# Spare TensorE products at the start, and two loads on ScalarE's queue, in a two-layer hybrid block

## The chip, the cores and the metric

The kernel runs on one core of a Trainium2 chip. The metric is the device time of one execution in microseconds (us); the time of a kernel is the median of its runs. A core has a matrix engine (TensorE, PE in the profile; its weight loads stand apart as PEld), VectorE (DVE), ScalarE (ACT), GpSimd (POOL) and SyncE (SP), which issues the transfers from memory. Each engine takes its instructions strictly in the order in which they stand in its own line, and they wait for each other by semaphores.

## The reference

256 tokens of width 1024 go through two layers. Each layer is half a gated feed-forward step, a mixer (convolution with a state-space part in the first layer, dilated attention in the second) and another half feed-forward step, every one of them between two norms:

```python
for i in range(DEPTH):
    g = norm_g[i]
    h = h + 0.5 * rms_norm(swiglu(rms_norm(h, g[0]), ffn_w1[i, 0], ffn_w2[i, 0]), g[1])
    u = rms_norm(h, g[2])
    ...
    h = h + rms_norm(m, g[3])
    h = h + 0.5 * rms_norm(swiglu(rms_norm(h, g[4]), ffn_w1[i, 1], ffn_w2[i, 1]), g[5])
```

Only the beginning matters here: the norm of x with the weights `g[0]`, and the first two products of the first `swiglu`, with 256 gate and 256 up columns each.

## The kernel before, in words

**Work.** The tokens are two tiles of 128. All weights come from memory in float32, in units of 128 x 2048 (1 MB). Each unit is split into a high part `wh` (a copy in the type fp32r, by ScalarE) and a low part `wl` (the difference, by VectorE, or by GpSimd for some units), and so are the activations `x`. A product of two float32 matrices is then three products of parts: high x high, high x low, low x high (`mm3`, each 128x128 by 128x512).

**Beginning.** `run` loads the two halves of tile 0 of x, the identity matrix `ident` (64 KB), the first norm's weights `gain0` (4 KB, one column for each block of 128 features), the two halves of tile 1, and with `prefetch(2)` the first two weight units in pieces of 512 columns. All of these are issued by SyncE, one behind the other. Then `post_pre` norms each tile: ScalarE squares each half and sums it (`sumsq`; the squares themselves go to a tile `junk` that nobody reads), VectorE and GpSimd make the inverse root, VectorE scales (`y`), PE turns eight blocks of 128x128 by a product with `ident` (into the banks `t` and `c`, four each), ScalarE takes the high parts with the gain (`x<-t,gain`), and VectorE the low ones. The first two groups of products (banks `w`, two of them, one for each token tile) read the units 0 and 1, 24 products each. Behind each group stand an activation (`sg`) by ScalarE and a multiplication (`pt`) by VectorE that free the bank, and the third group needs the first one's bank. An activation of another kind needs a table load on ScalarE (`ACT_TABLE_LOAD`).

**Order.** The program is recorded first, and then a scheduler writes it: it plays the recorded operations through a table of costs (`cost`), takes on each engine the operation with the lowest rank among those that can start soonest, and also gives out the buffers. Ranks are the place in the recording, shifted by `moved(...)`. `FIRST_RANKS` shifts the conversions of the first two weight units. A waiting instruction holds up all that stands behind it on its engine. All instructions are issued from one line of the program (L633 in the profile of before), so its groups are told apart by the tiles' names: `w<-wh,x` is a product of `wh` and `x` into a bank `w`.

Of the kernel before, what the change touches and what calls it, by code (L numbers as in the profile page):

```python
# [13 lines left out]
BF16 = mybir.dt.bfloat16  # L14
# [5 lines left out]
P = 128  # L20
# [4 lines left out]
KB = D // P  # L25
# [17 lines left out]
AFTER = 0  # L43
WIDE = (6, 8)
FIRST_PIECES = (512, 512)
FIRST_RANKS = (-1950, -1950)
SECOND = 30
POOL_PIECE = 512
ON_POOL = (1, 1, 1)
SHARED = (0, 3)  # L50
SHARED_RANKS = (2000, 500)
# [156 lines left out]
C_ID, C_ORDER, C_TAB = 0, P, 3 * P  # L208
# [4 lines left out]
N_CHAN = 340  # L213
# [88 lines left out]
class Recorder:  # L302
# [182 lines left out]
    def one_schedule(self):  # L485
# [55 lines left out]
        while len(order) < len(ops):  # L541
            for e in stale:
                best[e] = choose(e)
            stale = set()
            picks = [(b[3], e) for e, b in best.items() if b]
            assert picks, "no operation can start"
            e = min(picks)[1]
            s, o = best[e][1:3]
            cands[e].remove(o)
            stale.add(e)  # L550
            for b in o.bufs:
                if b.slot is None:
                    kind = b.kind
                    times = sorted((t, i) for i, t in enumerate(kind.free_at) if t is not None)
                    b.slot = next(i for t, i in reversed(times) if t + GAP <= s)
                    kind.free_at[b.slot] = None
                    b.prev = kind.tenant.get(b.slot); kind.tenant[b.slot] = b
                    while kind.first < len(kind.bufs) and kind.bufs[kind.first].slot is not None:
                        kind.first += 1
                    left[b] = len(b.uses)  # L560
                    b.last = 0.0
            length = o.cost
            if e == "scalar" and o.table:
                if o.table != table:
                    length += TABLE_LOAD
                table = o.table
            if o.shares_port:
                length += max(0.0, port - s)
                held = s + length
            if e == "gpsimd":  # L570
                length += max(0.0, held - s)
                if o.takes_port:
                    port = s + length
            if o.before_pow and s > FIXED:
                quiet = s + length + QUIET
            free[e] = s + length
            if e == "sync":
                bus = max(bus, s + DMA_START) + o.tail
                end[o.index] = bus + DMA_LATENCY
            elif o.name == "dma_start":  # L580
                bus = max(bus, s + ADD_START) + o.tail
                end[o.index] = bus + ADD_LATENCY
            else:
                end[o.index] = s + length
            o.start, o.end = s, end[o.index]
            order.append(o)
            for b in o.bufs:
                b.last = max(b.last, end[o.index])
                left[b] -= 1
                if not left[b]:  # L590
                    b.kind.free_at[b.slot] = b.last
                    stale = set(free)
            for u in users[o.index]:
                n = ops[u]
                ready[u] = max(ready[u], end[o.index] + latency(o, n, n.deps[o.index]))
                waits[u] -= 1
                if not waits[u]:
                    cands[n.engine].append(n)
                    stale.add(n.engine)
# [55 lines left out]
def cost(op, out):  # L655

    kw = op.kw
    op.table = None
    op.shares_port = op.takes_port = False
    n = out.free_size() if isinstance(out, View) else 0  # L660
    if op.engine == "tensor":
        stationary = op.args[1]
        if op.name == "transpose":
            return 109.0, 0.0
        if stationary.ap.dtype == F32R:
            return n / 2.4 + 13.5 if n > 256 else 114.0, 0.0
        if PAIRED and (stationary.ap.ap[0][1] == 64 or stationary.free_size() == 64):
            return max(2 * n / 2.4 + 5.0, 110.0), 0.0
        return 2 * max(2 * n / 2.4 + 2.5, 112.0), 0.0
    psum = any(isinstance(a, View) and a.buf.kind.psum for a in (*op.args, *kw.values()))  # L670
    if op.engine == "scalar":
        op.table = TABLES.get(op.args[2])
        views = sum(isinstance(kw.get(k), View) for k in ("bias", "scale")) + ("accum_out" in kw)
        filled = 115.0 if isinstance(out, View) and out.buf.kind.psum else 0.0
        return 0.832 * n + (52.0 if psum else 96.0) + 93.0 * views + filled, 0.0
    if op.engine == "gpsimd":
        if op.name == "memset":
            return 100.0, 0.0
        if op.name == "dma_start":
            return ADD_START, n * P * 4 / ADD_RATE  # L680
        if n == 1:
            return 515.0, 0.0
        op.takes_port = True
        spread = any(isinstance(v, View) and v.ap.ap[-1][0] == 0 for v in kw.values())
        return (1.95 if spread else 2.26) * n + (10.0 if spread else 92.0), 0.0
    if op.engine == "vector":
        op.shares_port = not psum
        if op.name == "tensor_scalar" or op.name == "tensor_copy":
            return (0.52 if not psum else 1.04) * n + (70.0 if n < 64 else 130.0), 0.0
        if op.name == "scalar_tensor_tensor":  # L690
            return 1.03 * n + (130.0 if n > 64 and isinstance(kw.get("scalar"), View) else 75.0), 0.0
        if op.name == "bn_aggr":
            return 200.0, 0.0
        if op.name in ("tensor_reduce", "bn_stats"):
            n = op.kw["in_"].free_size()
        return 1.042 * n + 67.0, 0.0
    dst = kw["out"]
    cols = dst.free_size() if isinstance(dst, View) else kw["in_"].free_size()
    return 475.0, cols * P * 4 / 300.0
# [23 lines left out]
class Kernel:  # L723
# [58 lines left out]
        self.nc.scalar.activation(hi, src, AF.Copy)  # L782
        (engine or self.nc.vector).tensor_tensor(out=lo, in0=src, in1=hi.bitcast(F32), op=ALU.subtract)

    def prefetch(self, upto):
        while self.next_unit < min(upto, len(self.plan)):
            i = self.next_unit
            parts, whole, more, how, piece = self.plan[i]
            step = FIRST_PIECES[i] if i < len(FIRST_PIECES) else 2048

            def raw_of(name):
                key = (parts[name[0]], name[1])
                if key not in self.raws:
                    a = self.raws[key] = self.slot([P, 2048], tag="raw")
                    for c in range(0, 2048, step):
                        self.nc.sync.dma_start(out=a[:, c : c + step], in_=self.weights[key[0]][:, c : c + step])
                return self.raws[key]

            raw = raw_of(whole)
# [9 lines left out]
            with self.nc.moved(FIRST_RANKS[i] if i < len(FIRST_PIECES) else LATE):  # L809
                engine, step = (self.nc.gpsimd, POOL_PIECE) if i == 1 or i - self.hybrid_at in GPSIMD_UNITS else (self.nc.vector, piece)  # L810
                if i < len(FIRST_PIECES):
                    step = FIRST_PIECES[i]
# [109 lines left out]
    def sumsq(self, acc, src, scale):  # L922
        junk = self.slot([P, 512], BF16, "junk")
        self.nc.scalar.activation(junk, src, AF.Square, scale=scale, accum_out=acc)

    def post_pre(self, t, y, half, gpost, gpre, xT, last=False):

# [5 lines left out]
    def _post_pre(self, t, y, half, gpost, gpre, xT, last):  # L933
        nc = self.nc
        f = 2.0 if half else 1.0
        h = self.h[t]
        hs = [slice(hf * 512, (hf + 1) * 512) for hf in range(2)]
# [8 lines left out]
        s2 = self.sm(2) if gpre is not None else None  # L946
        for hf in range(2):
            if y is not None:
                nc.vector.scalar_tensor_tensor(out=h[:, hs[hf]], in0=yg[hf], scalar=r, in1=h[:, hs[hf]], op0=ALU.mult, op1=ALU.add)
            if last:  # L950
                nc.sync.dma_start(out=self.out[t * P : (t + 1) * P, hs[hf]], in_=h[:, hs[hf]])
            if gpre is not None:
                self.sumsq(s2[:, hf : hf + 1], h[:, hs[hf]], 1 / 32.0)
                if y is not None:
                    nc.vector.tensor_tensor(out=yg[hf], in0=h[:, hs[hf]], in1=gpre[:, hs[hf]], op=ALU.mult)
        if gpre is None:
# [718 lines left out]
    def run(self):  # L1675
# [6 lines left out]
            (self.ffn, True),  # L1682
        ]
        xT = self.transposed_tile()
        load = self.nc.sync.dma_start
        for hf in range(2):
            c = slice(hf * 512, (hf + 1) * 512)
            load(out=self.h[0][:, c], in_=self.x[0:P, c])
        load(out=self.ident, in_=self.consts[:, C_ID : C_ID + P])
        load(out=self.gain0, in_=self.in_small[0][:, N_CHAN : N_CHAN + KB])  # L1690
        for hf in range(2):
            c = slice(hf * 512, (hf + 1) * 512)
            load(out=self.h[1][:, c], in_=self.x[P : 2 * P, c])
# [68 lines left out]
```

## Time and profile before

| | |
|---|---|
| median of three runs | 1057.73 us (1057.48, 1057.73, 1058.43) |
| the profiled execution | 1058.54 us, of which 1056.8 us from the first to the last instruction |
| PE busy | 1040.7 us (98%) |
| DVE, ACT, POOL busy | 934.9, 706.4, 193.1 us |
| read from memory | 194.5 MB, 185 GB/s over the span |

The timeline's rows give the start and the length of a merged row of equal instructions, the engine, the operation with its tiles, and the count; in brackets the idle time before it and who ended it. A row's length runs from the first start to the last end, and products overlap, so a product's step is read from the starts of rows. Times count from the first instruction.

### The profile page before, as it was taken

To read this page: it belongs to the slowest core of one execution; us is meant where nothing else is said; L and a number is where in the kernel's file an instruction comes from. 1 tells how busy PE (TensorE), PEld (TensorE's weight loads), DVE (VectorE), ACT (ScalarE), POOL (GpSimd) and SP (SyncE) were. 2 spreads that over 40 slices of the span, in tenths; PEclk is the share of its full clock that TensorE was granted. 3 is DMA by queue.
4 is the path that set the end of the run, shared out by engine and by line. 5 is a ranking of instruction groups with operands and counts; after the bars stand their busy time and mean duration, and the time that the engine had idled before them with its cause. 6 is when DMAs were issued, how large, how long until landed. Compare 5 with 4: busy or idle time off the path is not lost.

```text
span 1056.8 us, 14986 instructions
## 1 busy us (share of the span) xinstructions
PE 1040.7 (98%) x5426; PEld 871.1 (82%) x5426; DVE 934.9 (88%) x1525; ACT 706.4 (67%) x1327; POOL 193.1 (18%) x171
## 2 busy tenths in 40 slices
PE   6999999999999999999999999999999999999997
PEld 5888888899878888888888888888888788888886
DVE  4799997789999899999979999997688769999993
ACT  6756766679776685756766667586577657575671
POOL 2410000199995030000003000000000413000000
PEclk9999999999999999999999999999999999999999
DMA  9572657455332633754743557393755231475451
GB/s 334 202 276 108 252 200 278 160 172 183 124 104 96 239 120 139 263 222 173 288 173 138 182 216 262 109 345 136 266 180 180 100 121 60 158 261 216 162 199 40
DMA packets 30633, 196.51 MB, mean 186 GB/s; under 512 B 3680, under 2 KB 4576, under 8 KB 8032
## 3 DMA queue, kind: packets, MB, share of 16 engines
q1 hardware_dynamic: 30560, 195.57, 50.8%
q8 instruction: 42, 0.69, 0.3%
q14 instruction: 31, 0.25, 0.1%
HBM read 194.51 MB, written 1.05 MB: 185 GB/s over the span
## 4 chain that ended last, share of the span: by engine, by line
PE 94%; ACT 3%; DVE 1%; issue 1%; DMA 1%; SPq 0%; DVEq 0%; POOLq 0%; POOL 0%; ACTq 0%
PE w L633 40%; PE a L633 32%; PE t L633 12%; PE c L633 10%; ACT wh L633 1%; ACT s L633 1%; DMA raw<-in_weights 1%; ACT junk L633 0%; DVE wl L633 0%; ACT L633 0%; SPq L633 0%; DVE s L633 0%; ACT x L633 0%; DVE h L633 0%; DVE c L633 0%
## 5 line engine op out<-in xcount | busy, mean ns | idle before, releaser
L633 ACT ACTIVATE wh<-raw 128x512 fp32r<-128x512 f32 (+1 forms) x626 | 452.5, 775 | 145.0 <-DVE raw L633 49.3
L633 DVE TENSOR_TENSOR wl<-raw,wh 128x512 fp32r<-128x512 f32 (+1 forms) x554 | 483.5, 920 | 35.2 <-ACT wh L633 32.5
L633 PE MATMUL a<-wh,s 128*128 128x512 f32 x800 | 255.6, 391 | 0.0
L633 PE MATMUL w<-wh,x 128*128 128x512 f32 x600 | 197.5, 401 | 1.7 <-ACT x L633 1.2
L633 PEld LDWEIGHTS a<-wh,s 128*128 128x128 f32 x800 | 149.6, 188 | 32.2 <-ACT s L633 0.9
L633 PE MATMUL a<-wl,s 128*128 128x512 f32 x400 | 155.8, 390 | 0.0
L633 PE MATMUL w<-x,wh 128*128 128x512 f32 (+1 forms) x512 | 143.8, 348 | 0.1
L633 POOL TENSOR_TENSOR m<-m,mhalf 128x1 f32<-128x1 f32 x28 | 16.6, 594 | 694.0 <-DVE m L633 694.0
L633 PEld LDWEIGHTS w<-wh,x 128*128 128x128 f32 x600 | 112.5, 189 | 27.0 <-ACT x L633 1.9
L633 PE MATMUL w<-wl,x 128*128 128x512 f32 x300 | 118.9, 397 | 0.0
L633 PE MATMUL w<-x,wl 128*128 128x256 f32 x400 | 112.5, 281 | 0.0
L633 DVE TENSOR_TENSOR raw<-raw,raw 128x1024 f32<-128x1024 f32 (+1 forms) x104 | 110.0, 1087 | 0.1
L633 PEld LDWEIGHTS w<-x,wh 128*128 128x128 f32 x512 | 88.5, 189 | 12.2 <-DVE pt L633 0.5
L633 POOL TENSOR_TENSOR wl<-raw,wh 128x512 fp32r<-128x512 f32 x72 | 90.9, 1303 | 18.5 <-ACT wh L633 18.4
L633 PEld LDWEIGHTS a<-wl,s 128*128 128x128 f32 x400 | 75.1, 188 | 15.1
L633 PE MATMUL w<-wh,s 128*128 128x512 f32 x264 | 86.8, 390 | 0.0
L633 PEld LDWEIGHTS w<-x,wl 128*128 128x128 f32 x400 | 75.5, 189 | 1.3 <-issue 1.0
L633 PEld LDWEIGHTS w<-wl,x 128*128 128x128 f32 x300 | 56.9, 190 | 12.1 <-issue 0.6
L633 PEld LDWEIGHTS w<-wh,s 128*128 128x128 f32 x264 | 49.6, 188 | 10.7 <-ACT s L633 0.5
L633 PE MATMUL t<-x,wh 128*128 128x512 f32 x160 | 57.9, 397 | 0.0
L633 PE MATMUL c<-x,wh 128*128 128x512 f32 x160 | 56.6, 393 | 0.0
L633 DVE SCALAR_TENSOR_TENSOR t<-cv,chan,t 128x254 f32<-128x254 f32 (+29 forms) x112 | 52.3, 467 | 3.6 <-ACT t L633 3.2
(202 smaller groups left out, 1554.7 us busy)
## 6 DMA issues: line engine op xcount, KB each, us to landing
raw<-in_weights SPq DMA_DIRECT2D x176, 1024.0 KB, 4.9
g<-in_gains SPq DMA_DIRECT2D x11, 512.0 KB, 4.8
raw<-in_weights SPq DMA_DIRECT2D x8, 256.0 KB, 5.9
h<-in_x SPq DMA_DIRECT2D x4, 256.0 KB, 3.3
out<-h SPq DMA_DIRECT2D x4, 256.0 KB, 2.0
g<-in_consts SPq DMA_DIRECT2D x3, 192.0 KB, 2.4
chan<-in_chan SPq DMA_DIRECT2D x1, 170.0 KB, 9.4
order<-in_consts SPq DMA_DIRECT2D x1, 128.0 KB, 9.6
```

Of the source, the lines that this page charges most:

```text
L633: o.ins = f(*[real(a) for a in o.args], **{k: real(a) for k, a in o.kw.items()})
```

## The change

- `SPARES`: PE gets products of a 128x128 bf16 tile `spare` of zeros, which GpSimd clears at the start, into a bank `a` that nobody reads. Thirty come first, with the tile as both operands. After the first square of tile 0 come 8, after the second 12, after the second square of tile 1 another 6; these read 128 columns of the square's `junk` tile as an operand, so that they wait for the square, and a later square that takes the same `junk` buffer waits for them.
- `ident` and `gain0` are issued from ScalarE's own queue (`nc.scalar.dma_start`), ahead of its table load, and no longer by SyncE.
- `FIRST_RANKS`: the conversions of unit 1 get the rank shift -600 in place of -1950. `prefetch` has a new argument `beside` that no call uses. The table of costs learns the new kinds.

```diff
-FIRST_RANKS = (-1950, -1950)
+FIRST_RANKS = (-1950, -600)
...
+SPARES = (30, 8, 12, 0, 6)
...
     def sumsq(self, acc, src, scale):
         junk = self.slot([P, 512], BF16, "junk")
         self.nc.scalar.activation(junk, src, AF.Square, scale=scale, accum_out=acc)
+        return junk[:, 0:P]
+
+    def spares(self, count, moved):
+
+        for _ in range(count):
+            self.nc.tensor.matmul(self.bank[:, 0:P], self.spare, moved, start=True, stop=True)
...
-                self.sumsq(s2[:, hf : hf + 1], h[:, hs[hf]], 1 / 32.0)
+                junk = self.sumsq(s2[:, hf : hf + 1], h[:, hs[hf]], 1 / 32.0)
+                if y is None:
+                    self.spares(SPARES[1 + 2 * t + hf], junk)
...
         xT = self.transposed_tile()
+        self.spare = self.keep("spare", [P, P], BF16)
+        self.nc.gpsimd.memset(self.spare, 0.0)
+        self.bank = self.ps([P, 512], "a")
+        self.spares(SPARES[0], self.spare)
         load = self.nc.sync.dma_start
         for hf in range(2):
             c = slice(hf * 512, (hf + 1) * 512)
             load(out=self.h[0][:, c], in_=self.x[0:P, c])
-        load(out=self.ident, in_=self.consts[:, C_ID : C_ID + P])
-        load(out=self.gain0, in_=self.in_small[0][:, N_CHAN : N_CHAN + KB])
+        beside = self.nc.scalar.dma_start
+        beside(out=self.ident, in_=self.consts[:, C_ID : C_ID + P])
+        beside(out=self.gain0, in_=self.in_small[0][:, N_CHAN : N_CHAN + KB])
```

How the instructions stand now. PE, from the program's start to the first products, before (`t` and `c` are the turns of a tile's first and second half, `w` the products; the first two rows are tile 0, `t_228` is tile 1):

```order
L633 MATMUL t_186<-ident_64,y_0_69 128x128 x4
L633 MATMUL c_193<-ident_64,y_1_70 128x128 x4
L633 MATMUL w_207<-wh_123,x_73 128x512
L633 MATMUL w_207<-wl_74,x_73 128x512
L633 MATMUL w_207<-wh_123,x_73 128x512 x2
L633 MATMUL t_228<-ident_64,y_0_77 128x128 x4
```

PE at the same place now; of each run of spares (30, 8, 12, 6 pairs of a weight load and a product) one pair is shown:

```order
L634 LDWEIGHTS spare_124
L634 MATMUL a_165<-spare_124 128x128
...
L634 MATMUL a_165<-junk_67,spare_124 128x128
...
L634 MATMUL a_165<-junk_69,spare_124 128x128
L634 MATMUL t_240<-ident_63,y_0_71 128x128 x4
...
L634 MATMUL a_165<-junk_235,spare_124 128x128
L634 MATMUL c_260<-ident_63,y_1_73 128x128 x4
L634 MATMUL w_269<-wh_123,x_75 128x512
```

The first turn has fifty spares ahead of it. The turns of tile 1 moved too: the first four from behind four products to behind eight, and the second four from behind 26 products to behind 15. Now ScalarE, from its first instruction on, before:

```order
L633 ACT_TABLE_LOAD
L633 ACTIVATE junk_67,m_0_147<-h_0_63 128x512
...
L633 ACTIVATE wh_123<-raw_66 128x512
L633 ACTIVATE x_73<-t_186,gain_0_132 128x128 x2
L633 ACTIVATE x_76<-t_186,gain_0_132 128x128 x2
L633 ACTIVATE wh_123<-raw_66 128x512 x3
L633 ACTIVATE x_79<-c_193,gain_0_132 128x128 x2
```

And ScalarE now:

```order
L634 DMA ident_63<-in_consts 128x128
L634 DMA gain_0_134<-in_chan 128x8
L634 ACT_TABLE_LOAD
L634 ACTIVATE junk_67,m_0_149<-h_0_64 128x512
...
L634 ACTIVATE wh_123<-raw_66 128x512
L634 ACTIVATE x_75<-t_240,gain_0_134 128x128 x2
L634 ACTIVATE wh_123<-raw_66 128x512
L634 ACTIVATE x_78<-t_240,gain_0_134 128x128 x2
L634 ACTIVATE wh_123<-raw_66 128x512 x2
```

Two issues stand ahead of the table load, and the second weight piece (`wh<-raw`) stands between the high parts of x. VectorE follows that order, before:

```order
L633 TENSOR_TENSOR wl_74<-raw_66,wh_123 128x512
L633 TENSOR_SCALAR y_0_77<-h_0_65,m_3_201 128x512
L633 SCALAR_TENSOR_TENSOR x_73<-t_186,gain_0_132,x_73 128x128 x2
L633 SCALAR_TENSOR_TENSOR x_76<-t_186,gain_0_132,x_76 128x128 x2
L633 TENSOR_TENSOR wl_74<-raw_66,wh_123 128x512
```

And VectorE now:

```order
L634 TENSOR_TENSOR wl_76<-raw_66,wh_123 128x512
L634 TENSOR_SCALAR y_0_77<-h_0_65,m_3_254 128x512
L634 TENSOR_TENSOR wl_76<-raw_66,wh_123 128x512
L634 SCALAR_TENSOR_TENSOR x_75<-t_240,gain_0_134,x_75 128x128 x2
L634 TENSOR_TENSOR wl_76<-raw_66,wh_123 128x512
```

A second low weight piece stands ahead of the first low parts of x. Behind the first 48 products the order is the same but for some 50 instructions on PE, ScalarE and VectorE that changed places with a near neighbour.

More of the change, by code (lines that the diff above doesn't have):

```diff
@@ L576, in one_schedule @@
             free[e] = s + length
-            if e == "sync":
+            if e == "sync" or e == "scalar" and o.name == "dma_start":
                 bus = max(bus, s + DMA_START) + o.tail
@@ L664, in cost @@
             return 109.0, 0.0
+        if stationary.ap.dtype == BF16:
+            return 107.0 if op.args[2].buf.kind.name == "spare" else 60.0, 0.0
         if stationary.ap.dtype == F32R:
@@ L670, in cost @@
     psum = any(isinstance(a, View) and a.buf.kind.psum for a in (*op.args, *kw.values()))
+    if op.name == "dma_start" and op.engine == "scalar":
+        return 450.0, out.free_size() * P * 4 / 300.0
     if op.engine == "scalar":
@@ L783, in split, with prefetch @@
         (engine or self.nc.vector).tensor_tensor(out=lo, in0=src, in1=hi.bitcast(F32), op=ALU.subtract)
-    def prefetch(self, upto):
+    def prefetch(self, upto, beside=None):
         while self.next_unit < min(upto, len(self.plan)):
@@ L795, in raw_of @@
                     for c in range(0, 2048, step):
-                        self.nc.sync.dma_start(out=a[:, c : c + step], in_=self.weights[key[0]][:, c : c + step])
+                        (beside if beside and not c else self.nc.sync.dma_start)(out=a[:, c : c + step], in_=self.weights[key[0]][:, c : c + step])
                 return self.raws[key]
```

## The prediction

> **What bounds the kernel now.** I read the page first: its first row gives the span, its second and fourth the busy time of TensorE (PE) and VectorE (DVE).
>
> ```profile
> span 1056.8 us, 14986 instructions
> ...
> PE 1040.7 (98%) x5426; PEld 871.1 (82%) x5426; DVE 934.9 (88%) x1525; ACT 706.4 (67%) x1327; POOL 193.1 (18%) x171
> ```
>
> PE is idle for 1056.8 - 1040.7 = 16.1 us. The windows tell where: busy time of PE, PEld, DVE, ACT and POOL in turn, then the granted clock, the DMA share and GB/s.
>
> ```profile
> 0.00:25.06 25.06, 16.80 (x65) 13.00 (x65) 11.87 (x31) 17.02 (x41) 6.45 (x11) 1.00 0.91 331
> 25.06:50.00 24.94, 24.81 (x127) 20.84 (x128) 18.99 (x25) 19.34 (x35) 11.64 (x10) 1.00 0.61 215
> 50.00:100.00 50.00, 50.00 (x253) 42.32 (x252) 48.28 (x54) 30.47 (x43) 4.86 (x3) 1.00 0.48 178
> 100.00:170.00 70.00, 69.95 (x337) 58.55 (x336) 67.23 (x89) 49.48 (x75) 0.00 (x0) 1.00 0.67 254
> 1050.50:1056.80 6.30, 0.00 (x0) 0.00 (x0) 2.23 (x4) 0.69 (x2) 0.55 (x1) 0.69 0.22 83
> ```
>
> Of the 16.1 us, 8.26 lie before 25.06 and 6.30 behind the last product; 1.5 are left for 1025 us between. So whatever the first 25 us are shortened by ends the run earlier by as much, if nothing behind takes it back. The chain that ended last shows what that beginning waits for, in order of time:
>
> ```profile
> 2.58 0.43 SPq L633
> ...
> 3.53 5.29 DMA raw<-in_weights
> ...
> 9.78 2.38 PE w L633 x4
> ...
> 20.78 2.08 ACT wh L633 x4
> ...
> 22.87 1.28 ACT L633
> 24.17 0.39 ACT sg L633
> ...
> 24.58 0.43 DVE pt L633
> ...
> 25.06 5.10 PE w L633 x21
> ```
>
> SyncE's issues, the first weight piece (landed at 8.82), conversion, products; then from 20.78 a detour over ScalarE's conversions, its table load and the gate, until the third group of products starts at 25.06. The timeline of PE shows that the first products also run slowly (start, time of the row, count at the end):
>
> ```profile
> 6.78 1.11 PE L633 MATMUL t<-ident,y 128*128 128x128 f32 x4 [6.78 <-DVE y L633]
> 7.69 1.06 PE L633 MATMUL c<-ident,y 128*128 128x128 f32 x4
> ...
> 13.24 1.48 PE L633 MATMUL w<-wh,x 128*128 128x512 f32 x3
> 14.53 0.98 PE L633 MATMUL w<-wl,x 128*128 128x512 f32 x2
> 15.34 0.62 PE L633 MATMUL w<-wh,x 128*128 128x512 f32 x2
> ...
> 19.00 0.60 PE L633 MATMUL c<-ident,y 128*128 128x128 f32 x4
> 19.36 0.70 PE L633 MATMUL w<-wh,x 128*128 128x512 f32 x2
> 19.89 0.39 PE L633 MATMUL w<-wl,x 128*128 128x512 f32 x1
> ```
>
> From 13.24 to 14.53 three products take 0.43 us each. In a later stretch this window, PE alone, holds 19 that start in it (a twentieth began before): 18 steps in 4.10 us, 0.228 each.
>
> ```profile
> 20.12:24.24 4.12, 4.12 (x20) 1.00 1.00 373
> ```
>
> Turns go from 0.23 (four from 6.78 to 7.69) to 0.109 ((19.89 - 19.00 - 2 x 0.228) / 4). Both halve at about 15.3: a clock that is let go then, though the clock column already reads 1.00 over 0 to 25.06. It came 8.5 us after the first turn and 5.5 after the first product.
>
> **The change part by part.** The sum is made inside the profiled execution (1058.54 us, span 1056.8, so 1.7 outside), and asks when the third group of products, now at 25.06, can start.
>
> *Two loads to ScalarE's queue.* Rows of SyncE's queue, of ScalarE's table load and of the squares:
>
> ```profile
> 1.64 0.42 SPq L633 DMA_DIRECT2D ident<-in_consts  x1
> 2.11 0.43 SPq L633 DMA_DIRECT2D gain<-in_chan  x1
> ...
> 0.73 1.28 ACT L633 ACT_TABLE_LOAD   x1 [0.73 <-PEq L1752]
> 3.77 0.63 ACT L633 ACTIVATE junk<-h 128x512 bf16<-128x512 f32 x1 [1.76 <-DMA h<-in_x]
> 5.99 0.63 ACT L633 ACTIVATE junk<-h 128x512 bf16<-128x512 f32 x1 [0.74 <-DMA h<-in_x]
> ```
>
> Everything behind them on SyncE is issued 2.58 - 1.64 = 0.94 us earlier. The bytes stay, so the first weight piece comes 0 to 0.94 earlier than 8.82. I take 0.65: the second tile of x waits for its issue (0.74 idle before the square at 5.99), but the small packets still pass. So it lands at 8.17. On ScalarE the two issues push the table load to 0.73 + 0.94 + 1.28 = 2.95; the square at 3.77 hides that by 0.8. Identity is wanted at 6.78, the gains at 8.7; both land in time even at a landing time of 4 us. Two weight pieces now wait on the semaphores of these loads; their bytes queue behind earlier pieces, cost nothing.
>
> *Spares.* GpSimd clears the constant behind its first memset at 0.73, so PE starts at 1.1. No bf16 product of 128 columns is in the trace. Bounds: a quarter of the slow 512-column step, 0.43 / 4 = 0.107 us, and the slow f32 turn, 0.23. [...] Then 30 end at 4.3; 8 wait for the first square (3.77 + 0.63 = 4.4) and end at 5.3, 12 end at 6.6, ahead of the turn at 6.78: nothing is moved by them. [...] What they bring is the clock: with the two delays above it is free at 1.1 + 5.5 = 6.6 to 1.1 + 8.5 = 9.6.
>
> A wait is added: ScalarE's third square waits until PE has read the junk tile, 5.3 to 5.6, and behind it queue the fourth square and all conversions. The square now starts at 5.99, so it is covered as long as 38 spares stay under 0.13 each.
>
> *The new order of conversions.* After the first piece (rows: conversion 8.84, high parts of x 9.38; VectorE 9.51, 10.12, 10.54):
>
> ```profile
> 8.84 0.63 ACT L633 ACTIVATE wh<-raw 128x512 fp32r<-128x512 f32 x1 [1.38 <-DMA raw<-in_weights]
> 9.38 1.13 ACT L633 ACTIVATE x<-t,gain 128x128 fp32r<-128x128 f32 x4
> 9.51 0.69 DVE L633 TENSOR_TENSOR wl<-raw,wh 128x512 fp32r<-128x512 f32 x1 [1.80 <-ACT wh L633]
> 10.12 0.48 DVE L633 TENSOR_SCALAR y<-h,m 128x512 f32<-128x512 f32 x1
> 10.54 1.13 DVE L633 SCALAR_TENSOR_TENSOR x<-t,gain,x 128x128 fp32r<-128x128 f32 x4
> 10.95 1.22 PE L633 MATMUL w<-wh,x 128*128 128x512 f32 x2
> 14.28 5.04 POOL L633 TENSOR_TENSOR wl<-raw,wh 128x512 fp32r<-128x512 f32 x4 [5.87 <-ACT wh L633]
> 19.64 1.14 ACT L633 ACTIVATE x<-c,gain 128x128 fp32r<-128x128 f32 x4 [2.85 <-PE c L633]
> ```
>
> The third product needs the low parts of x: 10.95 - 8.84 = 2.11 us after the conversion. One low weight piece now stands ahead of them on VectorE (0.61, from 9.51 to 10.12), so 2.72; from 8.19 that is 10.9. Behind it everything is there when its turn comes: 46 products x 0.228 = 10.49 and 8 turns x 0.109 = 0.87, so the third group at 22.26. GpSimd starts its four low pieces at about 12.95 (8.19 + 4 conversions x 0.52 + 8 high parts x 0.25 + one conversion) and ends them at 18.0; the last is wanted at 19. The turns of the second tile's second half stand far earlier, so ScalarE no longer idles 2.85 us for them. Its conversions of the third unit wait for PE to leave the first unit's buffer: 10.9 + 24 x 0.228 + 0.87 + 0.4 = 17.6, then 2.1, 1.3, 0.4 and 0.4 for conversions, table, gate and multiply: 21.8. So the gate is no longer waited for, by 0.4 us.
>
> Sum: 22.26 - 25.06 = **-2.8 us**: 0.65 from the loads, some 2.4 from the clock (ten products at 0.2 and four turns at 0.1), 0.6 from the gate, less 0.85 for the longer wait for the third product.
>
> *Behind it* the order is nearly the same. The four weight tiles issued from here on have slack:
>
> ```profile
> 19.49 8.86 SPq L633 DMA_DIRECT2D raw<-in_weights  x4
> 31.81 0.62 ACT L633 ACTIVATE wh<-raw 128x512 fp32r<-128x512 f32 x1
> ...
> raw<-in_weights SPq DMA_DIRECT2D x6, 1024.0 KB, 7.6
> ```
>
> 19.49 + 7.6 = 27.1 against a use at 31.81: 4.7 us, more than the 2.8.
>
> **Against the runs shown** (1057.48 to 1058.43, median 1057.73) the profiled execution is 0.81 slow. Is that noise in both kernels, the change gives 1057.73 - 2.8 = 1054.9; is it something that the change removes, 1058.54 - 2.8 = 1055.7. I forecast the middle, **1055.3 us**. A difference under 0.2% (2.1 us) is what a measurement of this kernel can't tell from none.
>
> **The rivals.**
>
> *The clock comes as late as now.* The constant is zero and PE may not count such products as work. Then PE runs at half its pace from 10.9 to 15.3 and loses 2.2 of these 4.4 us: -2.8 + 2.2 = -0.6 from the median, about 1057.1. For it: the first turns, too, did not free the clock for 8.5 us. Against: the 30 spares are dense, which nothing before 9.78 was.
>
> *The clock's phase.* The release may fall at another point in each execution. The slowest of four times is the profiled one; if its 0.81 is a late release, the median loses less now, and the gain against it is 2.8 - 0.8 = 2.0: 1055.7. For it: the four times spread by 1.06 us. Against: nothing says that the spread is in the beginning. [...] No row here shows a second phase.
>
> *The spares stand in the way (slower).* They are in PE's line ahead of the turn, and ScalarE's squares wait for them. At 0.23 each with a late clock 50 end at 1.1 + 11.5 = 12.6, the six others and the eight turns put the first product at 15.8, 6.0 later than 9.78; then come 5.5 us of slow products (13), 35 x 0.228 and 0.87: 30.2, that is +5 us, 1062.8. It decides from about 0.14 us a spare (5 / 56 = 0.09 less than 0.23) if the clock is late too. Against: 0.23 is an f32 price.
>
> *VectorE takes it back.* It is idle for only 1.7 of 50 us from 50 and 2.8 of 70 us from 100. If it can't move forward, PE meets its waits again, and 0 to 2 us of the gain stay: about 1056.9. Against: VectorE is idle for 6 of 25 us from 25 on, and the transfers have slack.
>
> **How the numbers follow.** Forecast 0.58, phase 0.12, late clock 0.13, VectorE 0.09, spares in the way 0.06, something else on the slow side 0.02. The forecast's own bounds: the first piece 0 to 0.94 earlier (gain 2.15 to 3.1), a spare at 0.16 (turn at 9.1, some 0.9 less), both readings of the 0.81. The range is 1053.9 to 1057.2, which takes in the late clock. Faster: nearly all of the forecast and part of the phase, 0.60; same 0.32; slower 0.08.
>
> **What would show it.** Right: spares at 0.107 from 1.1, halving before 9.6; turns at 6.8 to 7.0; first piece converted at about 8.2; no step over 0.25 among the products from 10.9 on; the third group at 22.3 with no wait for the gate; and the same 2.8 us at 100 us as at the end. Wrong: products at 0.43 behind 11; a first turn behind 7.5; a first conversion still at 8.8; new waits for VectorE's low parts between 50 and 170.

## The result and the profile after

| | before | after |
|---|---|---|
| median | 1057.36 us (10 executions, 1056.29 to 1058.54) | 1055.39 us (10 executions, 1054.84 to 1057.03) |
| ratio, 95% interval | | 0.9981 (0.9972 to 0.9989) |
| the profiled execution, its span | 1058.54, 1056.8 us | 1055.28, 1053.5 us |

The change makes the kernel faster by 1.97 us in the median, 0.19%, just under what the prediction called telling; the interval excludes a ratio of 1. One of the eleven executions of a later kernel, first30, took 1713.98 us at a granted clock of 0.567; its median below is that of the other ten. Between the two profiled executions the difference is larger, 3.3 us. This gap between 2.0 and 3.3 is the first thing to explain.

The page after, first row and PE's row:

```profile
span 1053.5 us, 15099 instructions
...
PE 1042.8 (99%) x5482; PEld 873.3 (83%) x5482; DVE 934.0 (89%) x1525; ACT 706.0 (67%) x1327; POOL 193.5 (18%) x172
```

PE is idle for 10.7 us instead of 16.1, but 3.4 + 1.7 + 0.5 us of its busy time is now spares. The windows, cut at the third group of products as before (at 21.83 now instead of 25.06):

```profile
0.00:21.83 21.83, 19.19 (x120) 15.83 (x121) 12.22 (x32) 17.31 (x41) 6.64 (x12) 1.00 0.93 338
21.83:50.00 28.17, 27.84 (x141) 23.16 (x140) 21.52 (x29) 22.08 (x38) 11.21 (x10) 1.00 0.63 242
...
1047.20:1053.50 6.30, 0.00 (x0) 0.00 (x0) 2.23 (x4) 0.69 (x2) 0.55 (x1) 0.72 0.22 83
```

25.06 - 21.83 = 3.23 us are won in the beginning, and the span is 3.3 shorter: what happens between changes little in sum, and the end (6.30 us without PE, as before) nothing. The start of PE's products, compared one by one in the two traces, leads by 3.39 us at 27 us, 2.86 at 107 and 3.32 at the last product. The timeline of PE, after:

```profile
1.03 3.38 PE L634 MATMUL a<-spare 128*128 128x128 bf16 x30 [1.03 <-POOL spare L634]
4.56 1.69 PE L634 MATMUL a<-junk,spare 128*128 128x128 bf16 x20 [0.15 <-ACT junk L634]
6.76 0.66 PE L634 MATMUL t<-ident,y 128*128 128x128 f32 x4 [0.51 <-DVE y L634]
7.45 0.49 PE L634 MATMUL a<-junk,spare 128*128 128x128 bf16 x6
7.78 0.61 PE L634 MATMUL c<-ident,y 128*128 128x128 f32 x4
8.52 0.50 PE L634 MATMUL w<-wh,x 128*128 128x512 f32 x1
8.99 0.50 PE L634 MATMUL w<-wl,x 128*128 128x512 f32 x1
10.28 0.73 PE L634 MATMUL w<-wh,x 128*128 128x512 f32 x2 [0.79 <-DVE x L634]
10.85 0.39 PE L634 MATMUL w<-wl,x 128*128 128x512 f32 x1
```

Thirty spares take 3.38 us, the next twenty only 1.69; the record of the granted clock begins at 5.47 us (before: at 15.28). The first turns take 0.66 us instead of 1.11, the first product 0.50 instead of 0.80, and from 10.28 on the longest product step is 0.31 (at 14.21). The chain that ended last in the first 30 us:

```profile
0.73 3.23 DMA ident<-in_consts
...
4.82 5.07 DMA raw<-in_weights
9.88 0.35 DVE x L634
...
10.28 1.66 PE w L634 x6
```

From 10.28 on it is PE alone: the detour over the table load and the gate, which stood in the chain before, is gone. Ahead of that the chain has to be read with care. It puts the low parts of x at 9.88 down to the weight piece that was issued at 4.82. But that piece lands only at 10.75; it shares a semaphore with the gains, and those landed at 4.68. Rows of VectorE and, the last, of ScalarE:

```profile
9.27 0.69 DVE L634 TENSOR_TENSOR wl<-raw,wh 128x512 fp32r<-128x512 f32 x1
9.88 0.60 DVE L634 SCALAR_TENSOR_TENSOR x<-t,gain,x 128x128 fp32r<-128x128 f32 x2
```

```profile
9.13 0.62 ACT L634 ACTIVATE x<-t,gain 128x128 fp32r<-128x128 f32 x2
```

What ends just before the low parts of x is VectorE's second low weight piece (9.96, the instructions overlap a little) and ScalarE's second pair of high parts (9.75).

### The profile page after: what moved, and what is told of

Read it like the earlier page. It is cut to its first block, busy times and chain, and to the rows that moved or that the text cites. A ratio compares the mean times of both kernels' runs of the same rounds, so it can differ in the third digit from the quotient of the medians.

```text
span 1053.5 us, 15099 instructions
## 1 busy us (share of the span) xinstructions
PE 1042.8 (99%) x5482; PEld 873.3 (83%) x5482; DVE 934.0 (89%) x1525; ACT 706.0 (67%) x1327; POOL 193.5 (18%) x172
## 3 DMA queue, kind: packets, MB, share of 16 engines
HBM read 194.51 MB, written 1.05 MB: 186 GB/s over the span
## 4 chain that ended last, share of the span: by engine, by line
PE 96%; DVE 1%; ACT 1%; DMA 1%; issue 1%; SPq 0%; DVEq 0%; POOLq 0%; POOL 0%; ACTq 0%
PE w L634 41%; PE a L634 33%; PE t L634 12%; PE c L634 9%; DVE wl L634 1%; DMA raw<-in_weights 0%; ACT wh L634 0%; ACT junk L634 0%; DMA ident<-in_consts 0%; ACT s L634 0%; DVE s L634 0%; ACT L634 0%; DVE h L634 0%; DVE raw L634 0%; SPq L634 0%
```

## Experiments

**The kernel before, twice more.** No edit. Is the late release of the clock (15.28 us) a property of the kernel or of that execution?

> The kernel before once more, for one profile. My theory (the clock's phase): the slow steps of 0.43 us end at another point than 15.3, anywhere between 11.9 and 15.3, and the third group starts the earlier the sooner they end, 23.5 to 25.1; the span moves with it, by about 0.4 us for each us. Rival (noise elsewhere): third group at 25.0 to 25.1 again, and a span that differs from 1056.8 does so behind 25 us.

> The same kernel and the same expectations as the first look: by the phase theory a third point of release, with the third group between 23.5 and 25.1 and a span that follows it; by the rival the third group at 25.0 to 25.1.

Measured: 1056.33 and 1057.70 us. The timeline of PE in the first of the two:

```profile
9.36 0.68 PE L633 MATMUL w<-wl,x 128*128 128x512 f32 x1
9.93 1.18 PE L633 MATMUL w<-wh,x 128*128 128x512 f32 x2
10.94 0.60 PE L633 MATMUL t<-ident,y 128*128 128x128 f32 x4
...
22.66 0.50 PE L633 MATMUL w<-wh,x 128*128 128x512 f32 x1 [0.46 <-DVE pt L633]
```

Products and turns halve at 10.92 here, at 13.67 in the second repeat, at 15.28 in the profile of before. The third group starts at 22.66, 24.27 and 25.06, the spans are 1054.2, 1055.7 and 1056.8. So the beginning of the kernel before differs by 2.4 us from execution to execution, and the whole run follows it. The conversion of the first weight piece also starts at different times: 7.83, 8.76 and 8.84 us.

**Loads alone, spares alone.** The first has no spares, the second has the loads on SyncE again; both keep the new ranks, and the scheduler was left to lay out the rest. `...` marks lines left out, here and below.

```diff
 loads_alone
-SPARES = (30, 8, 12, 0, 6)
+SPARES = (0, 0, 0, 0, 0)
...
-        self.spare = self.keep("spare", [P, P], BF16)
-        self.nc.gpsimd.memset(self.spare, 0.0)
-        self.bank = self.ps([P, 512], "a")
-        self.spares(SPARES[0], self.spare)
 spares_alone
-        beside = self.nc.scalar.dma_start
+        beside = load
```

> The change without its spare products (no constant, no bank for them); identity and gains still go by ScalarE's queue, and the new rank shift stays. My theory: two parts, the clock and the earlier pieces. Without spares the clock is let go late, at some point between 11.9 and 15.3 us that differs from run to run; the first weight piece is converted at 7.6 as in the changed kernel, not at 8.84; the third group of products starts at 22 to 23.6, against 25.06 in the profile of before and 21.83 in that of the changed kernel. Time between the two kernels: 0.7 to 1.5 us under before, ratio 0.9987 to 0.9993, so within 0.2%. Rival, that the spares bring all of it: first piece near 8.8 or third group at 24.5 or later, ratio 0.9997 to 1.0005. Rival, that the loads bring all of it: ratio 0.998 like the full change.

> The change with identity and gains back on SyncE's queue where they were; the spares and the rank shift stay. My theory: clock let go at 5 to 9 us, first piece at 8.8 as before, no product slower than 0.25 us a step behind 11, no wait for the gate; third group at 22.5 to 23.0, that is 1.2 later than the changed kernel (the first piece's 1.27). Time 1.0 to 2.0 us under before, ratio 0.998 to 0.999. Rival, that the loads bring all of it: third group at 24.5 or later and ratio 0.9997 or more.

Measured, against one set of runs of before with median 1058.11: loads alone 1058.44, ratio 0.9999 (0.9990 to 1.0007); spares alone 1058.27, ratio 1.0000 (0.9991 to 1.0009). Neither half is worth anything by itself, so the simple picture, in which the parts add up, fell here. The spares alone do free the clock, at 4.82 us, but they lose it again, and not only in the profiled execution: 8 of the 11 have a mean granted clock of 0.995 to 0.997, while every profile here that kept its clock has 0.998 or more. Windows of that run (length, then PE, PEld, DVE, ACT, POOL; the granted clock is the third figure from the end):

```profile
1.41:4.82 3.41, 3.41 (x35) 3.41 (x33) 0.00 (x0) 1.94 (x5) 0.00 (x0) 1.00 0.75 233
4.82:8.23 3.41, 2.42 (x31) 1.97 (x28) 1.31 (x4) 1.95 (x5) 1.02 (x2) 1.00 0.85 280
8.23:11.64 3.41, 1.77 (x7) 0.97 (x6) 2.77 (x6) 2.98 (x10) 0.09 (x1) 1.00 0.98 300
11.64:15.05 3.41, 3.41 (x12) 2.73 (x11) 2.68 (x9) 2.73 (x10) 1.95 (x2) 0.50 1.04 428
```

In this run's records the clock changes only at instants that lie whole multiples of 3.41 us apart (the first three are 4.82, 11.64 and 15.05). Behind the window full of spares it is free; behind the next, in which PE was busy for 2.42 us, it stays so; behind the one with 1.77 us, in which PE waited 1.34 us for the low parts of x, the following 3.41 us run at 0.50. The third group starts at 24.06.

The loads alone have the late clock (14.16), start the third group at 23.58, 1.48 us ahead of the first profile, and lose that lead behind. Three rows of that run, of VectorE, GpSimd and PE:

```profile
68.43 1.34 DVE L634 TENSOR_TENSOR cv<-sg,sg 128x256 f32<-128x256 f32 x1 [0.38 <-ACT sg L634]
```

```profile
68.19 1.30 POOL L634 TENSOR_TENSOR cv<-v,v 128x512 f32<-128x512 f32 x1 [3.63 <-ACT wh L634]
```

```profile
88.81 0.50 PE L634 MATMUL c<-wh,s 128*128 128x512 f32 x1 [0.98 <-DVE sg L634]
```

A multiply that takes 0.42 us elsewhere in that run starts inside a GpSimd instruction and takes 1.34. VectorE has little slack between 66 and 110 us (42.15 of 44 us busy there), and PE waits 0.98 us for it at 88.81; at 107 us the lead is -0.17. This is the prediction's rival "VectorE takes it back", met in the profile of one half of the change. Why it is met there stays open. The chain of waits runs through the long multiply, but VectorE is as busy there in before (42.24 us) and in the changed kernel (42.41), and in both a low weight piece that starts inside the same GpSimd instruction takes longer (1.95 and 1.94 us instead of 1.22) without such a wait of PE.

**Without spares, in the same order.** Since the scheduler moves things when the spares go, the next kernels keep every engine's order of the changed kernel and only leave out or add spares when the program is written.

```diff
 mute
                 f = getattr(getattr(self.tc.nc, o.engine), o.name)
+                if o.engine == "tensor" and o.name == "matmul" and o.args[1].ap.dtype == BF16:
+                    continue
 first30: the same line with
+                ... and o.args[2].buf.kind.name == "junk":
```

> The changed kernel with every engine's order as it is, but without its 56 spare products (nothing of the result is left out). Loads and rank as changed. Theory (the spares bring the gain, by freeing the clock at 4.4 to 7.9 us instead of 10.9 to 15.3): the clock is freed between 10.5 and 14.5 us, the third group of products starts at 22.5 to 24.5, the ratio against the kernel before is 0.9985 to 1.0. Rival (the earlier loads and the order they bring are the gain, the spares are decoration): the third group at 21.8 to 22.2 and the ratio of the change, 0.9972 to 0.9989, with its middle at 0.998.

> The changed kernel with its order, and of the spares only the first 30 (3.38 us of TensorE work from 1.03 us); the 26 that multiply squares are not issued. Theory of windows (TensorE's clock is decided at instants 3.41 us apart whose phase differs from execution to execution, and is freed where nearly all of such a window was busy: 3.26 us of 3.41 was enough, 3.11 was not): 3.38 us fill a window only in about one execution of ten, so this run is like the one without spares, release at 10.5 to 14.5 us, third group at 22.5 to 24.5, ratio 0.9985 to 1.0. Rival (about 3 us of work in a row is enough whenever it comes): clock free by 5.5 us as in the changed kernel, third group at 21.8 to 22.4, ratio 0.9975 to 0.9985.

Measured on one chip, where before has 1058.22 and the changed kernel 1056.08 (below): mute 1058.00, ratio 0.9996 (0.9987 to 1.0005); first30 1057.98, ratio 0.9994 (0.9985 to 1.0004). So the spares are worth 1058.00 - 1056.08 = 1.9 us, and all of the gain is gone without them: ten of the eleven executions of mute lie at 1057.44 or above, nine of the eleven of the changed kernel at 1056.38 or below. The timeline of PE in mute:

```profile
9.31 0.79 PE L636 MATMUL w<-wh,x 128*128 128x512 f32 x1 [0.47 <-ACT x L636]
...
15.94 1.40 PE L636 MATMUL w<-wh,x 128*128 128x512 f32 x3
17.17 0.39 PE L636 MATMUL w<-wl,x 128*128 128x512 f32 x1
```

Its clock comes at 17.1, later than I had expected (10.5 to 14.5) and later than in any profile of before: the windows from 6.86 and from 10.27 on hold only 2.92 us of work each, with a wait of 0.50 us ahead of the third product in the second of them; the third group starts at 25.37. The first thirty spares alone give this (windows):

```profile
1.15:4.56 3.41, 3.26 (x30) 2.99 (x29) 0.00 (x0) 2.02 (x4) 0.00 (x0) 1.00 0.76 251
4.56:7.97 3.41, 1.09 (x8) 0.86 (x8) 1.10 (x3) 1.43 (x5) 0.56 (x1) 1.00 0.90 271
7.97:11.38 3.41, 1.37 (x3) 0.67 (x3) 2.35 (x6) 3.41 (x10) 0.56 (x1) 0.50 1.04 372
```

They free the clock at 4.56 and it is lost at 7.97, for two windows (to 14.80), after a window in which PE was busy for 1.09 us. I had expected such a release in one execution of ten; four of ten show the profiled one's mean granted clock of 0.995, so it is commoner. The verdict on the time holds: what the 26 spares behind the squares do here is keep the clock. In the changed kernel's profile the two windows behind the release hold 2.74 and 2.62 us of work (5.47 to 8.88 and 8.88 to 12.29), and the clock stays at 1.00.

**More spares where PE still idles.** Four more ahead of the first turn, ten between the second and the third product:

```diff
+            n = 0
...
+                if o.engine == "tensor" and o.name == "matmul":
+                    n += 1
+                    if o.args[1].ap.dtype == BF16:
+                        spare = o
+                    for _ in range({50: 4, 58: 10}.get(n, 0)):
+                        f(real(spare.args[0]), real(spare.args[1]), real(spare.args[1]), start=True, stop=True)
```

> The changed kernel with its order and 14 more spares where TensorE idled: 4 behind the 50 that stand ahead of the first turn (idle 0.51 us there) and 10 between the second product and the third (idle 0.79 us there). Theory of windows: from 1.03 to 10.3 us TensorE is then busy nearly without a gap, so that every phase has a full window; the clock is freed between 4.4 and 7.9 us in every execution and never lowered again; third group at 21.6 to 22.3, ratio 0.9970 to 0.9981, and no execution is more than 1.2 us above the fastest. Rival (the changed kernel's slow executions come from the loads, not from the clock): the same ratio and the same spread of about 2.2 us as the changed kernel's. Second rival (the added spares stand in the way of the first turn or the third product): third group 0.3 to 0.6 us later than the changed kernel's on the same chip.

> The changed kernel once more, on the same chip as the three others. Ratio 0.9972 to 0.9989 again. Theory of windows: its 5.1 us of spares in a row hold a whole window for about six phases of ten, so some executions are freed late (10 us or more) or, where a window from about 8.5 us on holds more than 1.3 us of idle time, lowered again for 3.41 us; the highest execution is 1.5 to 3 us above the lowest. Rival (the spares free it in every execution): all executions within 1 us of each other but for single ones that a load delays.

> The kernel with the 14 more spares once more, beside the three others on one chip. Theory of windows: as before, no slow execution: all within 1.2 us of the fastest, ratio 0.9965 to 0.9981. Rival (the narrow spread of its first runs was luck): one or more executions 1.5 to 3 us above the fastest, as 2 of 10 and 2 of 11 of the changed kernel's were.

Measured: filled 1055.70 (ratio 0.9974, 0.9964 to 0.9984) beside the changed kernel's 1056.08 (0.9983, 0.9974 to 0.9992) on the same chip; filled_again 1055.83 (0.9982, 0.9973 to 0.9991) on another, just outside what I had expected. The timeline of PE in filled:

```profile
6.69 0.39 PE L641 MATMUL a<-spare 128*128 128x128 bf16 x4
6.92 0.66 PE L635 MATMUL t<-ident,y 128*128 128x128 f32 x4
...
9.88 0.73 PE L641 MATMUL a<-spare 128*128 128x128 bf16 x10
10.83 0.72 PE L635 MATMUL w<-wh,x 128*128 128x512 f32 x2 [0.22 <-DVE x L635]
```

The third product waits 0.22 us in place of 0.79, with the spares in the gap. Counted from the first conversion, it comes 2.71 us and the third group 14.23 us later, the same as in the changed kernel (2.70 and 14.25): the 14 spares cost nothing. What they seem to change is the upper end. Of the changed kernel's 21 executions four lie 1.3 us or more above the middle (1056.82 and 1057.03; 1057.43 and 1058.02), and these four alone have a mean granted clock of 0.997, where the others have 0.998 to 1.000. None of the 19 with 14 more spares is at 0.997. That the four lost their clock for a window, as the spares alone did, is read from that column; no profile caught one. Four of 21 against none of 19 can also be chance, and a lost window lowers the mean by only 3.41 / 2 / 1054 = 0.0016, so that a 0.998 can hide one. The medians do not separate the two kernels: 0.38 us on one chip, with intervals that overlap. And my bound of 1.2 us on the spread failed on the second chip: 1056.65 - 1054.77 = 1.9, at an undisturbed clock. There the first weight piece is left as what varies.

**The loads, at a clock that is safe.** The filled kernel with the identity and the gains back on SyncE, in before's place, and all other orders kept:

```diff
+            beside = [o for o in order if o.name == "dma_start" and o.engine == "scalar"]
+            order = [o for o in order if o not in beside]
+            at = [i for i, o in enumerate(order) if o.engine == "sync"][2]
+            order[at:at] = beside
...
-                f = getattr(getattr(self.tc.nc, o.engine), o.name)
+                f = getattr(getattr(self.tc.nc, "sync" if o.name == "dma_start" and o.engine == "scalar" else o.engine), o.name)
...
```

> The kernel with the 14 more spares, every engine's order as it is, but the identity and the first norm weights back on SyncE, behind the first tile's two pieces and ahead of the second tile's, as in the kernel before. With the clock's phase out of the way this prices the loads alone. Theory (the prediction's term): the first weight piece is converted 0.65 to 1.3 us later than beside it, the time is 0.65 to 1.3 us above the kernel with the 14 spares (ratio 0.0006 to 0.0012 higher). Rival (the moment at which the first piece lands differs by up to 1 us from execution to execution in any case, and the two issues drown in it): less than 0.3 us.

Measured: 1056.54, ratio 0.9990 (0.9981 to 0.9998), 0.71 us above filled_again. The two intervals overlap a little, but all 11 executions lie above the median of filled_again. So the loads are worth about what the prediction took, but not where it put it. ScalarE's timeline in this run:

```profile
7.46 0.63 ACT L639 ACTIVATE wh<-raw 128x512 fp32r<-128x512 f32 x1
8.00 0.61 ACT L639 ACTIVATE x<-t,gain 128x128 fp32r<-128x128 f32 x2
9.52 0.63 ACT L639 ACTIVATE wh<-raw 128x512 fp32r<-128x512 f32 x1 [0.91 <-DMA raw<-in_weights]
```

The first piece is converted as early as ever (7.46); the second lands late, ScalarE waits 0.91 us for it, and the third product comes at 11.19, 3.73 us behind the first conversion instead of 2.7. In the new order it is the second piece on which the beginning hangs. The other profiles agree: the first piece lands at 7.94 us in the mean with the moved loads (nine profiles, 7.21 to 8.54) and at 8.10 with all loads on SyncE (five, 7.44 to 8.82), the second at 8.65 and 9.23. One of this kernel's 11 executions (1059.80, mean granted clock 0.996) seems to have lost the clock in that wait, in spite of the ten spares.

**The low parts of x first.** The prediction charged 0.85 us for a low weight piece that stands ahead of them on VectorE. Here it stands behind them (and 3 spares in the gap instead of 10):

```diff
+            v = [i for i, o in enumerate(order) if o.engine == "vector"]
+            low = order[v[6]]
+            order.insert(v[8] + 1, low)
+            order.pop(v[6])
...
```

> The kernel with the 14 more spares (3 of them between the second and the third product instead of 10), and on VectorE the two low parts of x that the third product waits for ahead of the second low weight piece instead of behind it. Theory (the order of the changed kernel is right as a whole, since the next product but one needs that low weight piece): the third product starts 0.3 to 0.8 us earlier after the first conversion, but the third group 0.3 to 0.6 us later (14.5 to 14.8 us behind the first conversion instead of 14.23), ratio 0.0003 to 0.0006 higher than beside it. Rival (the prediction's 0.85 us longer wait for the third product is a loss that can be had back): third group 13.4 to 13.9 us behind the first conversion, ratio 0.0004 to 0.0008 lower.

Measured: 1057.66, ratio 0.9998 (0.9989 to 1.0007), 1.83 us above filled_again; the third product 2.61 us behind the first conversion, the third group 15.68. Both theories were off, the rival in its sign and the other by three times. VectorE's timeline, and GpSimd's:

```profile
9.45 0.48 DVE L639 TENSOR_SCALAR y<-h,m 128x512 f32<-128x512 f32 x1
10.39 0.61 DVE L639 SCALAR_TENSOR_TENSOR x<-t,gain,x 128x128 fp32r<-128x128 f32 x2 [0.46 <-ACT x L639]
...
13.23 1.53 DVE L639 TENSOR_SCALAR y<-h,m 128x512 f32<-128x512 f32 x1
```

```profile
13.02 4.11 POOL L639 TENSOR_TENSOR wl<-raw,wh 128x512 fp32r<-128x512 f32 x3 [4.57 <-ACT wh L639]
```

With nothing ahead of them the low parts of x still start only at 10.39: VectorE idles 0.46 us for ScalarE, which ends the second pair of high parts at 10.35, behind the second weight piece. So the low weight piece filled a gap that was there anyway. Moved out of it, it pushes the rest of VectorE's queue back by some 0.5 us, past the start of GpSimd's work at 13.02, and the scaling `y` at 13.23 takes 1.53 us where the same instruction at 9.45 takes 0.48. Together these 0.5 and 1.05 us are of the size of the 1.45 by which the third group comes later behind the first conversion than in filled; that they are the cause is argued and not tried.

**Every spare twice.**

```diff
                 o.ins = f(*[real(a) for a in o.args], **{k: real(a) for k, a in o.kw.items()})
+                if o.engine == "tensor" and o.name == "matmul" and o.args[1].ap.dtype == BF16:
+                    o.ins = f(*[real(a) for a in o.args], **{k: real(a) for k, a in o.kw.items()})
```

> The changed kernel with its order and every spare product issued twice (112 instead of 56). Theory (a spare costs 0.107 us at the low clock and about 0.055 at the full one, and 60 + 40 of them stand ahead of the first turn): the first turn starts at 8.2 to 9.2 us instead of 6.8 to 7.4, the third group 1.0 to 2.0 us later than the changed kernel's for the same first conversion, ratio 0.9985 to 1.0. Rival (a spare stays at 0.107): 100 of them end at 11.7 us, the third group is 4 to 5 us later, ratio 1.002 to 1.003. Second rival (the spares hide in the wait for the loads whatever their number): no later, ratio 0.9970 to 0.9983.

Measured: 1056.88, ratio 0.9988 (0.9979 to 0.9997), 1.05 us above filled_again on the same chip; first turn at 8.15. Rows of PE, and one of ScalarE:

```profile
4.09 0.32 PE L636 MATMUL a<-spare 128*128 128x128 bf16 x1
4.20 0.26 PE L634 MATMUL a<-spare 128*128 128x128 bf16 x1
4.30 0.22 PE L636 MATMUL a<-spare 128*128 128x128 bf16 x1
4.36 0.22 PE L634 MATMUL a<-spare 128*128 128x128 bf16 x1
```

```profile
7.07 0.63 ACT L634 ACTIVATE junk<-h 128x512 bf16<-128x512 f32 x1 [1.52 <-PE a L636]
```

A spare's step is 0.107 us up to 4.30 and 0.055 behind it. Doubled, they stand in the way in just the place that the prediction named: ScalarE's third square waits 1.52 us until PE has read the junk tile, and the first conversion waits behind it: the piece landed at 7.22 and is converted at 8.45, where filled_again has 7.21 and 7.36. The price is some 1.1 us, not the 4 to 5 that a spare of 0.107 throughout would cost.

## Why the prediction was right, and where not

- **What bounds it.** Right: what the first 25 us lose, the whole run loses. In all fourteen profiles, with a third group anywhere from 21.6 to 25.4 us, the span is that start and 1031.4 to 1031.9 us, but for the loads alone (1033.1), which gave their lead back.
- **Spares at 0.107 us, then half; clock free by 9.6.** Right: 30 in 3.38 us, freed at 5.47, and at 4.41 to 6.55 in the other three profiles of these kernels; the rows of the doubled spares have 0.107 and 0.055. No run shows why a spare should take a quarter of the slow 512-column step, the bound that the forecast used; the runs show only that it does (0.107 against 0.43). That zeros might not count as work, the rival "late clock", is refuted: from 2.06 to 5.47, 3.26 of 3.41 us are products of zeros, and the clock is free behind them. Two of the prediction's signs were off, in small: the first conversion came at 7.58 us, not about 8.2, and a few product steps are over 0.25 (0.27 to 0.31).
- **The clock term, 2.4 us.** Right in mechanism; its size belongs to a draw. From the first conversion to the third group the kernel before took 16.22, 15.52 and 14.83 us at releases of 15.28, 13.67 and 10.92; the changed one takes 14.25. So the profiled pair gains 1.97 there, net of the longer wait for the third product and with the gate; the other two would gain 1.27 and 0.58. By medians the spares are worth 1.9 against the same order without them.
- **The loads, 0.65 us.** By medians 0.71. In the profiled pair 1.27 (7.58 against 8.84), outside my bounds of 0 to 0.94: the first conversion varies by itself, from 7.83 to 8.84 in before and from 7.36 to 8.19 with the moved loads and spares, and I took one draw for the place. The step that failed is the place: no shift of the first piece shows beside its own spread, the second piece comes earlier by some 0.6 us, and only the new order waits for it. That 0.65 was so near to 0.71 is in part luck.
- **The third product.** Forecast 2.72 us behind the first conversion, measured 2.70, by luck. The low weight piece on VectorE, which I gave as the cause, is worth only 0.1 us (2.61 with the piece behind the low parts): the low parts would wait for ScalarE's second pair as well, ahead of which the second weight conversion now stands. The list of the forecast's parts has 0.85 for this wait, but its rows give 2.72 - 2.11 = 0.61; and two of its ten slow products (9.78 and 10.37) lie ahead of the third, so nothing is saved behind it by them.
- **The gate.** Right: no wait at 21.83.
- **Against the median: the step that failed.** I took the middle between "noise in both" (gain 2.8) and "something that the change removes" (gain 2.0). The second was nearer. The profiled execution of before had the latest release of its three profiles and the latest first conversion. Against the second repeat, whose 1057.70 us lie nearest the median, its third group is 0.79 us later, and 0.70 of that arise behind the first conversion, where the clock is late. So the rival "the clock's phase" holds in the main, with its 2.0 against a measured 1.97, and my 0.12 for it was too low. That the forecast of 1055.3 met 1055.39 is luck: it was half of that rival already, the profiled pair gained 3.3 us and not 2.8, the median gain was 1.97 and not 2.4, and the median of before came out 0.37 below that of the three runs shown.
- **VectorE takes it back.** Small here (3.39 us of lead at 27 us, 2.86 at 107, and back to 3.32 at the end). In the profile of the loads alone it took back nearly the whole lead of 1.48.
- **Spares in the way.** Not at 56: they end 0.51 us ahead of the first turn. At 112 they cost some 1 us.

## What to carry to other kernels

Here the clock had to be freed and then kept: the thirty spares at the start brought nothing without the 26 that followed (1057.98 us, against 1058.00 with no spares and 1056.08 with all of them), and 14 more that fitted into waits cost nothing (the third group 14.23 us behind the first conversion, 14.25 without them). Before a beginning is priced from one profile, take profiles of two or three executions of the same kernel: in the three of before the clock was let go at 10.92, 13.67 and 15.28 us, and the first weight piece was converted at 7.83, 8.76 and 8.84. Keep the order fixed when one part of a change is taken out, or the scheduler's answer is measured along with it.

## What the runs showed of the hardware

- The stretches at full clock are multiples of one length in the traces' records: 1037.65 us in before, 1041.07 in both repeats, 1044.48 in after, that is 304, 305 and 306 times 3.413 us and 0.1; the low stretch in the spares alone is 3.413 us. The clock fell behind a window with 1.77 us of work and no wait over 1.34 us, and stayed behind one with 2.42 us (both in the spares alone); in first30 it fell behind one with 1.09 us.
- What a window needs to free the clock is not settled: it was free behind 3.10 us of spares in filled (3.14 to 6.55 us), and not behind 3.11 us of turns and products in the loads alone (7.34 to 10.75).
- Two VectorE instructions that start while GpSimd computes take three times as long as elsewhere in their runs: 1.53 us instead of 0.48 for the scaling (with the low parts of x first), 1.34 instead of 0.42 for the multiply (in the loads alone). The multiply ends 0.28 us behind the GpSimd instruction inside which it began (69.77 behind 69.49). Not all do this: the low parts of x behind that scaling take 0.34 us beside GpSimd, as elsewhere. In filled the scaling starts 0.31 us ahead of GpSimd's work (12.67 against 12.98) and keeps its 0.48; the one that takes 1.53 starts 0.21 us behind it (13.23 against 13.02).
